# Transposing q and k once, by pairs of heads, in a hybrid attention and convolution layer on one Trainium2 core

## The chip, the core and the metric

The kernel runs on one core of one Trainium2 chip. The metric is the device time of one execution in microseconds (us), the median of three runs. The engines are named as the profile names them: PE is TensorE's matmul stream and PEld its weight loads, DVE is VectorE, ACT is ScalarE, POOL is GpSimd, and SP is the engine whose queue issues nearly all DMAs.

## What is computed

One decoder layer on x of shape (1, 512, 1024) in float32. The reference, cut to what matters here:

```python
xn = rms_norm(h, g_mix_norm)
proj = xn @ w_in                       # 1024 x 2560
q, k, v, u = split(proj, [512, 1024, 1536])
q = partial_rope(to_heads(q)); k = partial_rope(to_heads(k))   # 8 heads of 64
attn = moba_attention(q, k, to_heads(v))       # 512 tokens, blocks of 256: causal softmax attention
conv = conformer_conv(u)               # GLU, causal depthwise conv of 31 taps, LayerNorm, swish
h = h + concat(attn, conv) @ w_out
h = h + square(relu(rms_norm(h) @ w_mlp_in)) @ w_mlp_out
return rms_norm(h)
```

With 512 tokens there are two blocks of 256, and the one earlier block is always chosen, so the attention is plain causal attention.

## The kernel before

Matmul operands are split into a high and a low part of the type fp32r, and a product is the sum of three matmuls (`mm3`, L267): high by high, high by low, low by high. The work has a front (norm, the projections u, q, k, v, the convolution, attention, the output projection y) and an MLP in four chunks (`ff`, `m`). This change is in the front.

The front is written as steps with an engine, a cost, needs and buffers. The class `Plan` lists them: again and again it takes, among the steps that can start, one that starts earliest by its own clock, and among equals the one with the longest tail of work plus a number from the table `BIAS`. Each engine then executes its instructions strictly in the listed order, waiting at each for what that one needs. So the table decides the order, and a late operand holds back everything that is listed behind its reader on that engine. SP is one such engine: a DMA that waits holds back the DMAs behind it.

The steps that matter here, per tile t of 128 tokens:

- `project` makes q, k and v in PSUM (96 matmuls of 512 columns each). `rope` copies a projection to SBUF on ACT (L649) and rotates a quarter of each head on DVE (L659 to L667). For q it writes each head twice, side by side (`dup = 2`), so one q tile has 1024 columns.
- `turn_q` transposes q on PE: for each t two groups of 4 heads (`tpq`, L682); each transposed head has its 64 dimensions in both halves of the partitions. ACT writes the high part `qs` (L687), DVE the low part `ql` (L691), one instruction each per group.
- `turn_k` transposes k by pairs of heads (`tpk`, L702): an even head lies in partitions 0 to 63, an odd one in 64 to 127. For one head `ks` holds the high part in one half of the partitions and the low part in the other; ACT (L707) and DVE (L710) write them for even and odd heads apart, on 64 partitions each.
- `attend`: a score tile (`s`, L775 to L777) is q high and q low against `ks`, 128 rows deep, so that high and low of k are summed in one pass. Then come the row maximum on DVE (`nm`, L782), exp on ACT (`pr`, L784), a reciprocal on DVE (`rs`), a scaling on POOL (L788), transposes of the probabilities on PE (`pt`, L793), their high part on ACT (`ph`, L798) and low part on DVE (`pl`, L802), and the product with v (`o`, L815, L816), which ACT and DVE gather (`ol`, `os`).
- The convolution is spread over DVE (`cs`, L572, one tap each), ACT and POOL. After its last tap `acc` (L589) is joined, PE transposes the sum (`cp`, L849), DVE and POOL normalize it (`bn`, `mv`, `r_ln`, `y` of L871), PE turns it back (`cb`) and ACT applies the swish (`yT`).
- The output projection `y` on PE serves as filler between attention's steps; its second half stands behind the plan, up to the first `ff` matmul.

Weights come by DMA into four `raw` tiles in turn (L446; unit n into tile n mod 4); ACT makes the high part `wh`, DVE or POOL the low part `wl` (L463). Units 12 to 15 are k's, 16 to 19 v's, 20 to 27 those of w_out.

The two lines that make the scores 128 rows deep:

```python
nc.tensor.matmul(p[:, 0:n], qs_tile()[:, h, tok], ks[:, h, 0:n], start=True, stop=False)
nc.tensor.matmul(p[:, 0:n], ql[:, h, tok], ks[:, h, 0:n], start=False, stop=False)
```

Of the kernel before, what the change touches and what calls it, by code (L numbers as in the profile page):

```python
# [17 lines left out]
P = 128  # L18
# [25 lines left out]
DVE_TAPS = (TAPS, 0, TAPS, 11)  # L44

BIAS = {
# [6 lines left out]
}  # L53
PSTEP = 384
PCOLS = 1664
# [116 lines left out]
def hybrid_layer(ctx: ExitStack, tc: tile.TileContext, x, pack, w_in, w_out, g_mlp, w1, w2, g_fin, out):  # L172
    nc = tc.nc
# [12 lines left out]
    def f32(ap):  # L186
        return ap.bitcast(F32)
# [234 lines left out]
    def ps_buffer(name):  # L422
        return plan.buffer("ps", lambda tag: psum.tile([P, 512], F32, tag=tag, name=name))
# [181 lines left out]
    own = [slice(0, HD), slice(HD, P)]  # L605
# [27 lines left out]

    def rope(nm, t, b, ready):


        dup = 2 if nm == "q" else 1
        r = rq[t] if nm == "q" else rs[t]
        qb = qpair[t // 2] if nm == "q" else new_pr(f"{nm}f{t}")

        def tile_of():
            f = get(qb)[t % 2] if nm == "q" else get(qb)
            return f[:, 0:dup * AW].rearrange("p (h u d) -> p h u d", h=NH, u=dup)

        def heads():
            return get(b).rearrange("p (h d) -> p h d", h=NH)

        def copy():
            nc.scalar.activation(tile_of(), heads().unsqueeze(2).to_broadcast([P, NH, dup, HD]), AF.Copy, scale=r)  # L649

        s = plan.step(f"cpy{nm}", "act", 0.69 if dup == 1 else 1.1, copy, needs=[ready], uses=[b, qb])

        def turn():

            two = 2 * HALF
            g = heads()
            cos, sin = (pk[:, c + t * two:c + (t + 1) * two].unsqueeze(1).to_broadcast([P, NH, two]) for c in (C_COS, C_SIN))
            rt = pa.tile([P, NH, two], F32, tag="rope", name=f"rt{nm}{t}", bufs=2)
            nc.vector.scalar_tensor_tensor(rt, g[:, :, 0:two], r, sin, op0=OP.mult, op1=OP.mult)  # L659
            nc.vector.scalar_tensor_tensor(g[:, :, 0:two], g[:, :, 0:two], r, cos, op0=OP.mult, op1=OP.mult)  # L660

            def part(x, n):
                return x[:, :, n * HALF:(n + 1) * HALF].unsqueeze(2).to_broadcast([P, NH, dup, HALF])

            q0, q1 = (tile_of()[:, :, :, n * HALF:(n + 1) * HALF] for n in range(2))
            nc.vector.tensor_tensor(q0, part(g, 0), part(rt, 1), op=OP.subtract)
            nc.vector.tensor_tensor(q1, part(g, 1), part(rt, 0), op=OP.add)  # L667

        s = plan.step(f"rope{nm}", "dve", 1.1, turn, needs=[s], uses=[qb, b])
        return qb, s  # L670

    qready, kready, q_hi = {}, {}, {}

    def turn_q(t, qb, s):
        ts = slice(t * P, (t + 1) * P)
        for a in range(2):
            tp = ps_buffer(f"tpq{t}{a}")

            def flip(a=a, tp=tp):
                for h in range(4):  # L680
                    c = (4 * a + h) * P
                    nc.tensor.transpose(get(tp)[:, h * P:(h + 1) * P], get(qb)[t % 2][:, c:c + P], ident)  # L682

            p = pe_step(f"tq{t}", 4 * 0.11, flip, needs=[s], uses=[qb, tp], chain=False)

            def high(a=a, tp=tp):
                nc.scalar.copy(qs_tile()[:, 4 * a:4 * a + 4, ts], get(tp).rearrange("p (a b) -> p a b", a=4))  # L687

            def low(a=a, tp=tp):
                hs = slice(4 * a, 4 * a + 4)  # L690
                nc.vector.tensor_sub(ql[:, hs, ts], get(tp).rearrange("p (a b) -> p a b", a=4), f32(qs_tile()[:, hs, ts]))  # L691

            hh = plan.step(f"qh{t}", "act", 0.59, high, needs=[p], uses=[tp])
            qready[t, a] = plan.step(f"ql{t}", "dve", 0.69, low, needs=[hh], uses=[tp])

    def turn_k(t, qb, s):
        ts = slice(t * P, (t + 1) * P)
        tp = ps_buffer(f"tpk{t}")

        def flip():  # L700
            for p in range(4):
                nc.tensor.transpose(get(tp)[:, p * P:(p + 1) * P], get(qb)[:, p * P:(p + 1) * P], ident)  # L702

        p = pe_step(f"tk{t}", 4 * 0.11, flip, needs=[s], uses=[qb, tp], chain=False)
        for a in range(2):
            def high(a=a):
                nc.scalar.copy(ks[own[a], a::2, ts], get(tp).rearrange("p (a b) -> p a b", a=4)[own[a]])  # L707

            def low(a=a):
                nc.vector.tensor_sub(ks[own[1 - a], a::2, ts], get(tp).rearrange("p (a b) -> p a b", a=4)[own[a]],  # L710
                                     f32(ks[own[a], a::2, ts]))

            hh = plan.step(f"kh{t}", "act", 0.59, high, needs=[p], uses=[tp])
            kready[t, a] = plan.step(f"kl{t}", "dve", 0.69, low, needs=[hh], uses=[tp])

    plan.slots("pt", ["pt0", "pt1"], 0.0)
    qpair = [plan.buffer("pt", lambda tag, i=i: [pa.tile([P, 2 * AW], F32, tag=f"{tag}{x}", name=f"qf{x}{i}") for x in "hl"])
# [44 lines left out]
    def attend(h):  # L762
# [3 lines left out]
        for qt in range(NT):  # L766
            n = (qt + 1) * P
            tok = slice(qt * P, n)
            sp, tp, pr = ps_buffer(f"s{h}{qt}"), ps_buffer(f"pt{h}{qt}"), new_pr(f"pr{h}{qt}")
            nm, sm, rc = (plan.buffer("st", lambda tag, x=x: perm.tile([P, 1], F32, tag=tag, name=f"{x}{h}{qt}"))  # L770
                          for x in ("nm", "sm", "rs"))

            def scores(sp=sp, n=n, tok=tok):
                p = get(sp)
                nc.tensor.matmul(p[:, 0:n], qs_tile()[:, h, tok], ks[:, h, 0:n], start=True, stop=False)  # L775
                nc.tensor.matmul(p[:, 0:n], ql[:, h, tok], ks[:, h, 0:n], start=False, stop=False)
                nc.tensor.matmul(p[:, tok], identb, maskb, start=False, stop=True)  # L777

            s = pe_step(f"sc{h}", 2 * mm(n) + 0.17, scores, uses=[sp], chain=False, keep=KEEP,
                        needs=[qready[qt, a]] + [kready[t, h % 2] for t in range(qt + 1)] + score_steps[-1:])  # L780
            score_steps.append(s)
            s = plan.step(f"max{h}", "dve", dve_cost(n), lambda sp=sp, nm=nm, n=n: nc.vector.tensor_reduce(  # L782
                get(nm), get(sp)[:, 0:n], AX.X, OP.max, negate=True), needs=[s], uses=[sp, nm])
            s = plan.step(f"exp{h}", "act", 0.45 + 0.00086 * n, lambda sp=sp, nm=nm, sm=sm, pr=pr, n=n: nc.scalar.activation(  # L784
                get(pr)[:, 0:n], get(sp)[:, 0:n], AF.Exp, bias=get(nm), accum_out=get(sm)), needs=[s] + lasts_exp[-1:], uses=[sp, nm, sm, pr])
            lasts_exp.append(s)
            s2 = plan.step(f"rec{h}", "dve", 0.15, lambda sm=sm, rc=rc: nc.vector.reciprocal(get(rc), get(sm)), needs=[s], uses=[sm, rc])
            s = plan.step(f"norm{h}", "pool", 0.32 + 0.00085 * n, lambda pr=pr, rc=rc, n=n: nc.gpsimd.tensor_scalar(  # L788
                get(pr)[:, 0:n], get(pr)[:, 0:n], get(rc), 1.0, op0=OP.mult, op1=OP.mult), needs=[s2], uses=[pr, rc])

            def flip(tp=tp, pr=pr, qt=qt):
                for j in range(qt + 1):
                    nc.tensor.transpose(get(tp)[:, j * P:(j + 1) * P], get(pr)[:, j * P:(j + 1) * P], ident)  # L793

            s = pe_step(f"tp{h}", (qt + 1) * 0.11 + 0.05, flip, needs=[s], uses=[tp, pr], chain=False)

            def high(tp=tp, qt=qt, n=n):
                nc.scalar.copy(key_tiles(get(pt)[0], qt), get(tp)[:, 0:n].rearrange("p (a b) -> p a b", b=P))  # L798

            def low(tp=tp, qt=qt, n=n):  # L800
                ph, pl = get(pt)
                nc.vector.tensor_tensor(key_tiles(pl, qt), get(tp)[:, 0:n].rearrange("p (a b) -> p a b", b=P),  # L802
                                        f32(key_tiles(ph, qt)), op=OP.subtract)

            s = plan.step(f"ph{h}", "act", act_cost(n), high, needs=[s], uses=[tp, pt])
            lows.append(plan.step(f"pl{h}", "dve", dve_cost(n), low, needs=[s], uses=[tp, pt]))
# [599 lines left out]
```

## Time and profile before

| | |
|---|---|
| median of 3 runs | 557.06 us (556.67 to 557.71) |
| the profiled execution | 557.05 us |
| its span, first to last instruction | 555.3 us |
| busy in the span: PE, DVE, ACT, POOL | 541.1, 447.9, 290.9, 214.8 us |
| mean granted TensorE clock | 0.993 |

The time of the profiled execution is 1.75 us over its span, which lies before the first and behind the last instruction. A busy time is the union of an engine's instructions; matmuls overlap, so the distance between two starts is what a matmul costs, not its length in the record. The front ends where the first `ff` matmul starts.

### The profile page before, as it was taken

The page shows a single profiled execution, that of the slowest core. Times are in us where ns is not written, and L with a number is a line of the kernel's source. Part 1 is how long each engine was busy: PE and PEld are TensorE (multiplying, and loading weights), DVE is VectorE, ACT ScalarE, POOL GpSimd, SP SyncE. Part 2 cuts the span into 40 slices and gives each one's busy share as a digit, 9 for nine tenths or more (in the row PEclk, how much of TensorE's full clock was granted, in tenths as well). Part 3 has the DMA queues.
Part 4 walks back from the last instruction along what each step waited for, and adds up shares of the span by engine and source line. Part 5 has one row for each costly group of instructions (what it writes and reads, how often), then busy time and mean ns, then how long its engine had stood idle before and what let it go on. Part 6 is the DMA issues. An engine that isn't in the chain of part 4 may idle for free.

```text
span 555.3 us, 7323 instructions
## 1 busy us (share of the span) xinstructions
PE 541.1 (97%) x2676; PEld 452.1 (81%) x2676; DVE 447.9 (81%) x613; ACT 290.9 (52%) x454; POOL 214.8 (39%) x186
## 2 busy tenths in 40 slices
PE   7999999999999999999999999999999999999993
PEld 6988888777778789988888888888888888888883
DVE  3499999999998577487999475999475999395996
ACT  5847497788883744343553334453244453245354
POOL 3219978777655511250050520240610330800454
PEclk8999999999999999999999999999999999999998
DMA  8552313220204261550027720028620048610003
GB/s 271 156 152 77 99 54 114 76 94 24 74 6 164 95 195 38 185 195 0 1 76 206 248 77 1 1 83 236 210 76 1 0 118 242 186 61 1 1 1 151
DMA packets 58835, 56.18 MB, mean 101 GB/s; under 512 B 1840, under 2 KB 42928, under 8 KB 58800
## 3 DMA queue, kind: packets, MB, share of 16 engines
q1 hardware_dynamic: 58512, 54.68, 31.5%
q10 hardware_dynamic: 288, 1.05, 0.5%
q8 instruction: 21, 0.34, 0.2%
q14 instruction: 14, 0.11, 0.1%
HBM read 53.62 MB, written 2.10 MB: 100 GB/s over the span
## 4 chain that ended last, share of the span: by engine, by line
PE 87%; DVE 8%; issue 1%; ACT 1%; DMA 1%; POOL 0%; SPq 0%; ACTq 0%; POOLq 0%
PE ff L270 11%; PE ff L269 11%; PE ff L271 10%; PE m L270 9%; PE m L269 9%; PE m L271 9%; PE u L270 3%; PE u L269 3%; PE u L271 3%; PE y L269 3%; PE y L271 2%; PE y L270 2%; DVE cs L572 2%; PE q L271 1%; PE q L270 1%
## 5 line engine op out<-in xcount | busy, mean ns | idle before, releaser
L269 PE MATMUL ff<-hTh,wh 128*128 128x512 f32 (+1 forms) x280 | 103.9, 371 | 0.0
L270 PE MATMUL ff<-hTl,wh 128*128 128x512 f32 (+1 forms) x280 | 103.8, 371 | 0.0
L271 PE MATMUL ff<-hTh,wl 128*128 128x512 f32 (+1 forms) x280 | 103.8, 371 | 0.0
L1067 POOL TENSOR_TENSOR r<-r,r 128x1024 f32<-128x1024 f32 x16 | 46.2, 2895 | 141.3 <-DVE wl L1059 136.5
L1075 ACT CAST wh<-raw 128x1024 fp32r<-128x1024 f32 x29 | 30.6, 1055 | 79.0 <-PE ff L270 59.0
L1075 ACT CAST wh<-r 128x1024 fp32r<-128x1024 f32 x40 | 41.7, 1051 | 44.7 <-POOL r L1067 25.7
L1059 DVE TENSOR_TENSOR wl<-raw,wh 128x1024 fp32r<-128x1024 f32 x29 | 39.9, 1375 | 29.4 <-ACT wh L1075 29.2
L1093 DVE TENSOR_TENSOR xr<-xr,m 128x512 f32<-128x512 f32 x96 | 59.5, 677 | 0.9 <-PE m L271 0.9
L269 PEld LDWEIGHTS ff<-hTh,wh 128*128 128x128 f32 x280 | 52.8, 188 | 9.1
L271 PEld LDWEIGHTS ff<-hTh,wl 128*128 128x128 f32 x280 | 52.7, 188 | 9.1
L270 PEld LDWEIGHTS ff<-hTl,wh 128*128 128x128 f32 x280 | 52.8, 188 | 9.0
L1067 POOL TENSOR_TENSOR t<-r,r 128x1024 f32<-128x1024 f32 x8 | 20.1, 2517 | 90.5 <-DMA r<-w 90.5
L572 DVE SCALAR_TENSOR_TENSOR cs<-hin,pk,cs 128x512 f32<-128x512 f32 x68 | 50.9, 749 | 1.0
L1059 DVE TENSOR_TENSOR wl<-r,wh 128x1024 fp32r<-128x1024 f32 x38 | 50.4, 1354 | 0.7 <-ACT wh L1075 0.7
L1110 DVE SCALAR_TENSOR_TENSOR F<-ff,rl 128x512 f32<-128x512 f32 x32 | 21.9, 686 | 33.8 <-ACT rl L1109 33.6
L556 POOL TENSOR_TENSOR acc<-acc,ct 128x512 f32<-128x512 f32 x30 | 44.4, 1479 | 6.5 <-ACT ct L553 4.5
L1109 ACT ACTIVATE rl<-ff 128x512 f32<-128x512 f32 x32 | 19.0, 594 | 49.0 <-PE ff L271 49.0
L553 ACT ACTIVATE ct<-hin,pk 128x512 f32<-128x512 f32 x49 | 32.9, 717 | 2.9 <-DVE hin L536 2.1
L459 ACT CAST wh<-raw 128x1024 fp32r<-128x1024 f32 x21 | 22.0, 1050 | 20.2 <-PE u L270 12.6
L463 DVE TENSOR_TENSOR wl<-raw,wh 128x1024 fp32r<-128x1024 f32 x18 | 29.4, 1633 | 0.9 <-ACT wh L459 0.9
L269 PE MATMUL u<-xh,wh 128*128 128x256 f32 (+1 forms) x88 | 29.6, 337 | 0.0
L270 PE MATMUL u<-xl,wh 128*128 128x256 f32 (+1 forms) x88 | 29.3, 333 | 0.0
(225 smaller groups left out, 1392.4 us busy)
## 6 DMA issues: line engine op xcount, KB each, us to landing
raw<-w SPq DMA_DIRECT2D x32, 512.0 KB, 4.0
r<-w SPq DMA_DIRECT2D x32, 512.0 KB, 5.6
raw<-w_in SPq DMA_DIRECT2D x18, 512.0 KB, 3.6
raw<-w_out SPq DMA_DIRECT2D x8, 512.0 KB, 3.7
xr<-x SPq DMA_DIRECT2D x4, 512.0 KB, 5.7
out<-ot SPq DMA_DIRECT2D x8, 256.0 KB, 2.1
x<-x SPq DMA_DIRECT2D x4, 256.0 KB, 4.8
raw<-w_in SPq DMA_DIRECT2D x4, 256.0 KB, 6.5
```

Of the source, the lines that this page charges most:

```text
L269: nc.tensor.matmul(ps, sh, mh, start=first, stop=False)
L270: nc.tensor.matmul(ps, sh, ml, start=False, stop=False)
L271: nc.tensor.matmul(ps, sl, mh, start=False, stop=last)
L459: nc.scalar.copy(hi, raws[n])
L463: e.tensor_tensor(lo, raws[n], f32(hi), op=OP.subtract)
L553: p = plan.step(f"prod{i}", "act", 0.72, lambda src=src, j=j, ct=ct: nc.scalar.activation(get(ct), src, AF.Copy, scale=wtap(i, j)), needs= ...
L556: s = plan.step(f"tapp{i}", "pool", 1.38, lambda ct=ct: nc.gpsimd.tensor_tensor(get(acc), get(acc), get(ct), op=OP.add), needs=[p, s], use ...
L572: s = plan.step(f"tapd{i}", "dve", 0.78, lambda src=src, j=j, last=last: nc.vector.scalar_tensor_tensor(get(acc) if last else get(cs), src ...
L1059: e.tensor_tensor(lo(), x(), f32(hi()), op=OP.subtract)
L1067: e.tensor_tensor(out(), a(), b(), op=op)
L1075: h = plan.step(f"{kind}h", "act", 1.04, lambda: nc.scalar.copy(get(wb)[0], get(b)), needs=[ready, last.get("high")], uses=[b, wb])
L1093: return plan.step("mev", "dve", dve_cost(n), lambda: nc.vector.tensor_tensor(xt[t][:, cols], xt[t][:, cols], get(b)[:, 0:n], op=op), need ...
```

## The change

q is no longer written twice (`dup = 1`). For each t one group of 4 transposes turns pairs of heads; ACT writes the high part of all four pairs into the even places of `qs` on 128 partitions, DVE the low part into `ql`. An even head then lies right in the lower half only, and the odd head of the pair lies in the upper half of the even head's place. DMAs from SBUF to SBUF carry the parts to their places, 64 partitions by 4 by 128 numbers each, 128 KB: `odd` fills both halves of the odd heads from the upper half of the even places (two DMAs), then `even` copies the lower half over the upper half. That is six DMAs for each t, three for `qs` and three for `ql`.

For k, ACT writes the high part of all pairs into the even places of `ks` and DVE the low part into the odd places, each once on 128 partitions. Then three DMAs follow one another: `side` puts the odd heads' high part away in the upper half of the tile `kf`, `even` moves the even heads' low part into the place that this leaves free, and `odd` brings the high part back from `kf`. Each waits for the one ahead of it. With 24 DMAs for q and 12 for k, 36 are new, all on SP. A score step now needs all parts of its q tile and of all k tiles up to its own.

The core of the diff:

```diff
-        dup = 2 if nm == "q" else 1
+        dup = 1
...
-        for a in range(2):
-            tp = ps_buffer(f"tpq{t}{a}")
...
+        tp = ps_buffer(f"tpq{t}")
+        def flip():
+            for p in range(4):
+                nc.tensor.transpose(get(tp)[:, p * P:(p + 1) * P], get(qb)[t % 2][:, p * P:(p + 1) * P], ident)
...
+        def high():
+            nc.scalar.copy(qs_tile()[:, 0::2, ts], get(tp).rearrange("p (a b) -> p a b", a=4))
...
+        def odd(m):
+            def fn():
+                for half in own:
+                    nc.sync.dma_start(f32(m()[half, 1::2, ts]), f32(m()[own[1], 0::2, ts]))
+            return fn
+        def even(m):
+            return lambda: nc.sync.dma_start(f32(m()[own[1], 0::2, ts]), f32(m()[own[0], 0::2, ts]))
+        oh = plan.step(f"qo{t}", "sp", 1.0, odd(qs_tile), needs=[hh, ll])
+        ol = plan.step(f"qo{t}", "sp", 1.0, odd(lambda: ql), needs=[ll])
+        eh = plan.step(f"qe{t}", "sp", 0.5, even(qs_tile), needs=[oh])
+        el = plan.step(f"qe{t}", "sp", 0.5, even(lambda: ql), needs=[ol])
+        qready[t] = [oh, ol, eh, el]
...
+            nc.scalar.copy(ks[:, 0::2, ts], get(tp).rearrange("p (a b) -> p a b", a=4))
+            nc.vector.tensor_sub(ks[:, 1::2, ts], get(tp).rearrange("p (a b) -> p a b", a=4), f32(ks[:, 0::2, ts]))
+        def side():
+            nc.sync.dma_start(get(qb)[own[1]].rearrange("p (a b) -> p a b", a=4), f32(ks[own[1], 0::2, ts]))
+        def even():
+            nc.sync.dma_start(f32(ks[own[1], 0::2, ts]), f32(ks[own[0], 1::2, ts]))
+        def odd():
+            nc.sync.dma_start(f32(ks[own[0], 1::2, ts]), get(qb)[own[1]].rearrange("p (a b) -> p a b", a=4))
+        s = plan.step(f"ka{t}", "sp", 0.5, side, needs=[hh, p], uses=[qb])
+        e = plan.step(f"kb{t}", "sp", 0.5, even, needs=[s, ll])
+        kready[t] = [e, plan.step(f"kc{t}", "sp", 0.5, odd, needs=[e], uses=[qb])]
...
-                        needs=[qready[qt, a]] + [kready[t, h % 2] for t in range(qt + 1)] + score_steps[-1:])
+                        needs=qready[qt] + [r for t in range(qt + 1) for r in kready[t]] + score_steps[-1:])
```

The table `BIAS` is new for the front; one entry of it, for example:

```diff
-    "norm": 442, "norm3": -13, "os": 124, "ph": 233, "pl": 174, "pl7": 41, "prod": -261, "projq": -117,
+    "mbh": -377, "mbl": -249.6, "mev": -240.1, "mfo": -646, "ml7": 207, "ms1": 261, "norm": 442, "ol": 208,
```

Three places where the order moved. First the SP queue between the weight loads of w_out. Before, only loads stand there (`raw20` is the tile of unit 20):

```order
L446 DMA raw20_1041<-w_out 128x2x512
L446 DMA raw21_1149<-w_out 128x2x512
L446 DMA raw22_1189<-w_out 128x2x512
L446 DMA raw23_1247<-w_out 128x2x512
L446 DMA raw24_1313<-w_out 128x2x512
```

Now the moves of k stand between them (L725 is `side`, L728 `even`, L731 `odd`; `kf1` is tile 1's, and so on; the rows begin behind the `side` of tile 1):

```order
L728 DMA ks_348<-ks_348 64x4x128
L731 DMA ks_348<-kf1_1054 64x4x128
L725 DMA kf2_1086<-ks_348 64x4x128
L445 DMA raw21_1143<-w_out 128x2x512
L728 DMA ks_348<-ks_348 64x4x128
L731 DMA ks_348<-kf2_1086 64x4x128
L445 DMA raw22_1173<-w_out 128x2x512
L725 DMA kf0_1027<-ks_348 64x4x128
L725 DMA kf3_1145<-ks_348 64x4x128
L445 DMA raw23_1231<-w_out 128x2x512
L728 DMA ks_348<-ks_348 64x4x128
L731 DMA ks_348<-kf0_1027 64x4x128
```

Tile 0, which the first score needs, comes third, behind tiles 1 and 2 and two weight loads.

Second, PE at the first score (`s00`). Before, it stands behind 42 of v's 96 matmuls and 28 transposes of q:

```order
L269 MATMUL v1_1134<-wh17_1110,xh_119 128x512
L270 MATMUL v1_1134<-wl17_1111,xh_119 128x512
L271 MATMUL v1_1134<-wh17_1110,xl_120 128x512
L775 MATMUL s00_1242<-ks_348,qs_828 128x128
L776 MATMUL s00_1242<-ks_348,ql_347 128x128
L777 LDWEIGHTS identb_105
```

Now it stands behind 63 of v's matmuls and 16 transposes of q:

```order
L268 MATMUL v1_1130<-wh18_1134,xh_119 128x512
L269 MATMUL v1_1130<-wl18_1135,xh_119 128x512
L270 MATMUL v1_1130<-wh18_1134,xl_120 128x512
L798 MATMUL s00_1285<-ks_348,qs_822 128x128
L799 MATMUL s00_1285<-ks_348,ql_347 128x128
L800 LDWEIGHTS identb_105
```

The first score moved 21 matmuls of v back and 12 transposes forward.

Third, DVE ahead of the first row maximum (`nm`). Before:

```order
L463 TENSOR_TENSOR wl18_1152<-raw18_945,wh18_1151 128x1024
L710 TENSOR_TENSOR ks_348<-tpk3_1159,ks_348 64x4x128 x2
L572 SCALAR_TENSOR_TENSOR cs2_822<-hin2_222,pk_65,cs2_822 128x512 x2
L710 TENSOR_TENSOR ks_348<-tpk0_1200,ks_348 64x4x128 x2
L463 TENSOR_TENSOR wl19_1198<-raw19_999,wh19_1197 128x1024
L691 TENSOR_TENSOR ql_347<-tpq30_1218,qs_828 128x4x128
L782 TENSOR_REDUCE nm03_1252<-s00_1242 128x1
```

Now:

```order
L462 TENSOR_TENSOR wl19_1194<-raw19_992,wh19_1193 128x1024
L722 TENSOR_TENSOR ks_348<-tpk0_1188,ks_348 128x4x128
L688 TENSOR_TENSOR ql_347<-tpq3_1196,qs_822 128x4x128
L722 TENSOR_TENSOR ks_348<-tpk3_1179,ks_348 128x4x128
L571 SCALAR_TENSOR_TENSOR cs2_820<-hin2_222,pk_65,cs2_820 128x512 x4
L462 TENSOR_TENSOR wl20_1261<-raw20_1034,wh20_1260 128x1024
L805 TENSOR_REDUCE nm03_1294<-s00_1285 128x1
```

A pair of low parts of k became one, and more taps (`cs`) stand ahead of the first maximum: between it and the join `acc` of the last channel group there were 22 taps and are now 17, and one `ql` fewer; the last `pl` of 512 columns moved from behind the join to ahead of it. On PE, the product with v of the last head moved ahead of the first `cp`, three `y` matmuls behind it, and the scores are all issued ahead of the first `y`. Behind the first `ff` matmul no engine's order changed.

## Rows read from the trace of the kernel before

**Rows 1.** Busy time by stretch of the front.
```profile
core 0: us, PE busy (x) PEld busy (x) DVE busy (x) ACT busy (x) POOL busy (x), PEclk, DMA share, GB/s
75.00:116.00 41.00, 40.58 (x201) 33.62 (x200) 39.65 (x67) 34.27 (x51) 32.12 (x24) 1.00 0.25 78
116.00:136.00 20.00, 19.89 (x113) 15.92 (x112) 19.87 (x43) 16.05 (x38) 13.56 (x15) 1.00 0.16 53
136.00:158.00 22.00, 20.80 (x137) 16.36 (x135) 21.88 (x62) 20.15 (x59) 14.18 (x20) 1.00 0.14 48
158.00:172.00 14.00, 13.98 (x82) 11.46 (x81) 13.94 (x33) 9.26 (x26) 6.01 (x10) 1.00 0.40 138
172.00:217.00 45.00, 44.94 (x229) 37.25 (x228) 30.91 (x43) 22.47 (x37) 16.08 (x24) 1.00 0.37 111
```
**Rows 2.** PE in order of time: start, length, instruction; transposes of q and k.
```profile
75.05 1.03 PE L682 MATMUL tpq<-ident,qfh 128*128 128x128 f32 x8
75.84 0.48 PE L269 MATMUL q<-wh,xh 128*128 128x512 f32 x1
76.15 0.40 PE L270 MATMUL q<-wl,xh 128*128 128x512 f32 x1
76.38 0.39 PE L271 MATMUL q<-wh,xl 128*128 128x512 f32 x1
...
101.35 0.39 PE L271 MATMUL k<-wh,xl 128*128 128x512 f32 x1
102.15 0.63 PE L702 MATMUL tpk<-ident,kf 128*128 128x128 f32 x4 [0.42 <-DVE kf L667]
```
**Rows 3.** PE: the first score, the first `cp`, the first `ff`.
```profile
116.80 0.22 PE L775 MATMUL s<-ks,qs 128*128 128x128 f32 x1
...
171.81 1.03 PE L849 MATMUL cp<-ident,acc 128*128 128x128 f32 x8
172.60 0.47 PE L815 MATMUL o<-ph,vhl 128*128 128x512 f32 x1
...
173.91 0.44 PE L269 MATMUL y<-wh,mixh 128*128 128x512 f32 x1
...
216.68 0.28 PE L269 MATMUL ff<-hTh,wh 128*128 128x256 f32 x1
```
**Rows 4.** DVE in order of time: first maximum, taps, the last join.
```profile
118.89 0.28 DVE L782 TENSOR_REDUCE nm<-s 128x1 f32<-128x128 f32 x1
119.09 0.75 DVE L572 SCALAR_TENSOR_TENSOR cs<-hin,pk,cs 128x512 f32<-128x512 f32 x1
119.74 0.16 DVE L787 RECIPROCAL rs<-sm 128x1 f32<-128x1 f32 x1
...
170.97 0.67 DVE L589 TENSOR_TENSOR acc<-more,cs 128x512 f32<-128x512 f32 x1
171.57 0.67 DVE L802 TENSOR_TENSOR pl<-pt,ph 128x512 fp32r<-128x512 f32 x1
```
**Rows 5.** Groups of DVE by line: busy us, mean ns, idle before.
```profile
L463 DVE TENSOR_TENSOR wl<-raw,wh 128x1024 fp32r<-128x1024 f32 x18 | 29.4, 1633 | 0.9 <-ACT wh L459 0.9
...
L710 DVE TENSOR_TENSOR ks<-tpk,ks 64x512 fp32r<-64x512 f32 x8 | 5.5, 688 | 0.2
...
L691 DVE TENSOR_TENSOR ql<-tpq,qs 128x512 fp32r<-128x512 f32 x8 | 5.2, 681 | 0.0
```
**Rows 6.** ACT in order of time around the first transposes of k.
```profile
102.82 1.18 ACT L707 CAST ks<-tpk 64x512 fp32r<-64x512 f32 x2 [0.35 <-PE tpk L702]
```
**Rows 7.** DMA issues of the whole span, from the page: KB each, us to landing.
```profile
out<-ot SPq DMA_DIRECT2D x8, 256.0 KB, 2.1
```
**Rows 8.** DMA issues from 27 to 30 us: one load in pieces of 512 bytes.
```profile
raw<-w_in SPq DMA_DIRECT2D x1, 512.0 KB, 3.6
```
**Rows 9.** Busy time by stretch while that load moved (columns as in rows 1).
```profile
28.00:31.00 3.00, 3.00 (x26) 3.00 (x26) 2.76 (x4) 1.15 (x2) 0.00 (x0) 1.00 0.61 175
```
**Rows 10.** SP's queue in order of time: the issue of one DMA.
```profile
0.79 0.38 SPq L284 DMA_DIRECT2D x<-x  x1
```

More of the change, by code (lines that the diff above doesn't have):

```diff
@@ L46 @@
 BIAS = {
[6 rows of a table removed]
+    "ct": 14, "high": 172, "kh3": -79, "low22": -126, "max": -27, "max1": 16, "max5": -83, "max6": -78,
+    "mbh": -377, "mbl": -249.6, "mev": -240.1, "mfo": -646, "ml7": 207, "ms1": 261, "norm": 442, "ol": 208,
[3 rows of a table added]
 }
@@ L675, in turn_q, with low @@
         ts = slice(t * P, (t + 1) * P)
-        for a in range(2):
-            tp = ps_buffer(f"tpq{t}{a}")
[L679 to L694, printed above, removed]
+        tp = ps_buffer(f"tpq{t}")
+        def flip():
+            for p in range(4):
+                nc.tensor.transpose(get(tp)[:, p * P:(p + 1) * P], get(qb)[t % 2][:, p * P:(p + 1) * P], ident)
+        p = pe_step(f"tq{t}", 4 * 0.11, flip, needs=[s], uses=[qb, tp], chain=False)
+        def high():
+            nc.scalar.copy(qs_tile()[:, 0::2, ts], get(tp).rearrange("p (a b) -> p a b", a=4))
+        def low():
+            nc.vector.tensor_sub(ql[:, 0::2, ts], get(tp).rearrange("p (a b) -> p a b", a=4), f32(qs_tile()[:, 0::2, ts]))
+        hh = plan.step(f"qh{t}", "act", 0.59, high, needs=[p], uses=[tp])
+        ll = plan.step(f"ql{t}", "dve", 0.69, low, needs=[hh], uses=[tp])
+        def odd(m):
[10 more added lines that the diff above has]
+        qready[t] = [oh, ol, eh, el]
     def turn_k(t, qb, s):
@@ L704, in turn_k, with high, low @@
         p = pe_step(f"tk{t}", 4 * 0.11, flip, needs=[s], uses=[qb, tp], chain=False)
[L705 to L714, printed above, removed]
+        def high():
+            nc.scalar.copy(ks[:, 0::2, ts], get(tp).rearrange("p (a b) -> p a b", a=4))
+        def low():
+            nc.vector.tensor_sub(ks[:, 1::2, ts], get(tp).rearrange("p (a b) -> p a b", a=4), f32(ks[:, 0::2, ts]))
[5 more added lines that the diff above has]
+            nc.sync.dma_start(f32(ks[own[0], 1::2, ts]), get(qb)[own[1]].rearrange("p (a b) -> p a b", a=4))
+        hh = plan.step(f"kh{t}", "act", 0.59, high, needs=[p], uses=[tp])
+        ll = plan.step(f"kl{t}", "dve", 0.69, low, needs=[hh], uses=[tp])
+        s = plan.step(f"ka{t}", "sp", 0.5, side, needs=[hh, p], uses=[qb])
+        e = plan.step(f"kb{t}", "sp", 0.5, even, needs=[s, ll])
+        kready[t] = [e, plan.step(f"kc{t}", "sp", 0.5, odd, needs=[e], uses=[qb])]
     plan.slots("pt", ["pt0", "pt1"], 0.0)
```

8 rows, old and new, of the table BIAS are left out of this document.

## The prediction

> **What bounds the kernel now.** Read the busy times by stretch first [rows 1]. TensorE is busy nearly all the time, and from the first score (116.80) to the first transposes of the convolution (171.81) VectorE is too: 19.87 of 20, 21.88 of 22 and 13.94 of 14 us. TensorE has room there and only there: 20.80 of 22 us from 136 to 158. The granted clock is 1.00 in every stretch, so neither engine's prices change with it. ScalarE (20.15 of 22 us at most) and GpSimd have room. So three things set the front's end in turn: TensorE up to the first score, VectorE from the first row maximum to the join of the last channel group, TensorE again from there to the MLP. TensorE in order of time shows the marks: scores from 116.80, `cp` at 171.81, `ff` at 216.68 [rows 3]; VectorE in order of time shows the first maximum at 118.89 and the join's end at 170.97 + 0.67 = 171.64, with `cp` right behind it [rows 4]. Behind the first `ff` the order is the old one on every engine, so the MLP takes its 339 us as before and only moves.
>
> The sum is made against the profiled execution, 557.05 us (span 555.3 and 1.75 around it), which is the median of the three runs to 0.01.
>
> **Term 1, TensorE up to the first score.** Twelve of the sixteen transposes of q that go stood ahead of it. Eight took from 75.05 to 75.84, and the matmul behind them 0.31 instead of 0.23 [rows 2]: 0.87 for eight, 0.109 each, 1.31 for twelve. The first transposes of k waited for VectorE's rope: from 101.35 to 102.15 are 0.80 instead of 0.23 [rows 2], 0.57 lost. VectorE has less ahead of that place (three `ql` of 0.68 [rows 5]) and TensorE comes 1.31 earlier; I take the 0.57 as gone. Against that, 21 more matmuls of v stand ahead of the score, 21 x 0.227 = 4.77; that work is only moved, for v has 96 matmuls in either kernel. TensorE is at the first score at 116.80 - 1.31 - 0.57 + 4.77 = 119.7.
>
> **Are the operands there?** This is the one new wait, and its price is in no row. SP issues in order. From the tail of the queue: tile 1's `side`, `even` and `odd`, tile 2's three, tile 0's three, with the loads of units 21, 22 and 23 between. Each `even` waits for its `side` to land and each `odd` for its `even`; what stands behind waits along. Up to the landing of tile 0's last part that is 7 landings in series. The start: tile 1's transposes at 102.15 - 1.31 - 0.57 = 100.3, ScalarE's copy begins 0.67 later and lasts 0.59 (102.82 and half of 1.18) [rows 6], so 101.6. Three issues lie between landings, 0.4 each [rows 10]: 1.2. Tile 0's moves queue behind loads: a load of 512 KB kept the 16 engines busy 0.61 x 3 = 1.8 us [rows 9], less the 0.4 between the issues is 1.4 for the first, and up to 0.7 for the second; I take 1.7 for both. So the operands are there at 104.5 + 7 L, with L the time from the issue of 128 KB to its landing, and TensorE does not wait as long as L is under 2.17.
>
> L is bounded from both sides. The stores of 256 KB, which also start in SBUF, took 2.1 [rows 7]; half as much should not take more. A load of 512 KB in pieces of 512 bytes, the moves' own piece size, took 3.6 [rows 8]; without three quarters of its 1.8 us of data that is 2.25. I take 2.1, the row nearest in source and size: the operands are there at 119.2, half a microsecond ahead of TensorE. The far end, 3.6, would put them at 129.7.
>
> The Trainium skill, page "DMA: Bandwidth & Descriptors", section "Anatomy of one DMA", gives a DMA a fixed 2.0 us and its bytes over 436 GB/s, most of the fixed part being the receipt of the last write; for 128 KB that is 2.3, as an estimate from the page. By it the first score would wait 0.9 us and the sum below would come to 556.3. The 2.1 measured for twice the bytes [rows 7] is under what that rule gives, 2.6; so here the trace speaks for less.
>
> The six moves per tile of q wait in the same way, and the loads of units 17 to 20 stand behind them; q's first transposes stand at 75.05, k's first at 102.15 [rows 2], and v's matmuls, which read unit 17, behind those; 27 us cover the three early rounds of moves of about 4 us each. If that cover fails, v waits and the first score with it.
>
> **Term 2, VectorE from first maximum to join.** VectorE would be free for the maximum at about the old 118.89: four `ks` (0.69) and three `ql` (0.68) go, 4.8, and six taps (119.74 - 119.09 = 0.65 each [rows 4]) and one weight split (1.63 [rows 5]) come, 5.5, and rope writes half as much. So the score decides: the maximum follows it by some 0.6, at 120.3. From there to the join it took 171.64 - 118.89 = 52.75, without idle time [rows 1]. Five taps less are 3.25; one `ql` less and one `pl` of 512 more (0.68 and 0.67) cancel. 120.3 + 52.75 - 3.25 = 169.8, that is 1.8 earlier. TensorE is not in the way: its own work there falls more, by 21 matmuls of v, a group of q's transposes and 3 of `y`, less the last head's product that comes in (1.31), some 4.6 in all. The pieces written on 128 instead of 64 partitions cost nothing extra: 688 ns on 64 and 681 on 128 [rows 5].
>
> **Term 3, from the join to the MLP.** TensorE runs through (44.94 of 45 [rows 1]). The last head's product, 172.60 to 173.91, is out of this stretch, 1.31, and three `y` come in, 0.69: 0.6 less. The weight split that GpSimd gives up stands behind the normalization on VectorE, which has 14 us of room here.
>
> **Nothing for the rest.** ScalarE loses eight copies of 0.59 [rows 6]; it waits for others anyway. The 36 moves are 36 x 0.45 (a quarter of 1.8) = 16 us of DMA time spread over some 50 us whose share was 0.25 [rows 1].
>
> **The sum**: -1.8 - 0.6 = -2.4. From it I take back 0.8. The taps that go were the work with which VectorE bridged the chain from maximum to exp to transposes to low part; 17 are left for 22, and TensorE has no `v` and no `y` between attention's steps for longer. The bounds are 0, the present state, and 3.25, if all five leave holes; present idle of nearly 0 is the nearer row, so a quarter. **557.05 - 2.4 + 0.8 = 555.4 us.**
>
> **Rivals.**
>
> *The chain of moves decides (slower).* If L is over 2.17, each 0.1 costs 0.7 us, since seven landings follow one another and VectorE is full from the first maximum on. At 2.41 the gain is gone, at 2.57 the kernel is 0.2% slower, at 2.7 the score stands at 123.4 and the time is 559.1. For it: the operands would be ready only 0.5 us ahead, and no row shows a move inside SBUF. Against it: 2.1 for double the size.
>
> *The bridge is gone (no change).* If the holes on VectorE take half or all of 3.25 instead of a quarter, the time is 556.2 to 557.9. For it: ScalarE at 20.15 of 22 us was close too, and the chain of a head passes four engines. Against it: VectorE had no holes with TensorE, ScalarE and GpSimd all less than full. The same holds if a low part on 128 partitions at the new stride took twice as long, 4 x 0.69 ahead of the maximum: 557 or so.
>
> *The saving doesn't reach the end.* If the first score comes early but the normalization of the convolution, which now stands in one piece, makes TensorE wait 1 or 2 us behind `cp`, the time is 556.4 to 557.4; 24 `y` matmuls between `cp` and `cb` cover 5.4 us, so I count it with the second rival.
>
> **How the numbers follow.** A measurement of this kernel can tell 0.2%, 1.1 us, from no change: faster is below 555.9, slower above 558.2. The forecast's case, moves in time and at most half of the holes, gets 0.53, and it lies from 553.9 (no holes is 554.6, and the estimates of the score's place and of the 0.6 to the maximum may be 0.7 too high together) to 555.9. The second and third rival together with the milder part of the first, L between 2.2 and 2.55, get 0.28. L above that gets 0.19. The range reaches from 553.9 to 558.4, L up to 2.6, and leaves out the worse tail. Faster 0.53, same 0.28, slower 0.19.
>
> **What would show it.** Right: the moves of 128 KB land within 2.2 us; PE has no idle time at the first scores; the first maximum comes near 120.3, the join ends near 170.5, the first `ff` starts 1.5 to 2 us earlier. Wrong: idle time of PE ahead of `s` released by a DMA (first rival); VectorE busy clearly under 99% between first maximum and join (second); PE idle ahead of `cb` (third). If the first score came before 119 with little idle, my constant of 104.5 would be too high, and the order of v alone would decide.

## The result, and the profile after

The changed kernel takes 560.35 us (median of 5 runs, 559.56 to 562.41) against 557.06 (5 runs too): ratio 1.0067, 95% interval 1.0051 to 1.0082. It is 0.67% slower; 555.4 was forecast. The profiled execution took 560.01 us with a span of 558.3.

The front's start differs from execution to execution by up to 2.5 us, so stretches are compared from one instruction, the first matmul of q, whose row in the kernel before is this (PE in order of time: start, length, instruction):

```profile
58.04 0.39 PE L269 MATMUL q<-wh,xh 128*128 128x512 f32 x1
```

In that kernel the fourth group of scores (the first of 512 columns) follows the work ahead of it without a stop:

```profile
123.77 0.23 PE L777 MATMUL s<-maskb,identb 128*128 128x128 bf16 x1
123.81 0.48 PE L775 MATMUL s<-ks,qs 128*128 128x512 f32 x1
```

The same view of the changed kernel, with q's first matmul, the first and the fourth group of scores, and `cp`:

```profile
57.58 0.39 PE L268 MATMUL q<-wh,xh 128*128 128x512 f32 x1
...
118.92 0.39 PE L270 MATMUL v<-wh,xl 128*128 128x512 f32 x1
121.40 0.30 PE L798 MATMUL s<-ks,qs 128*128 128x128 f32 x1 [2.09 <-issue]
...
125.38 0.27 PE L816 MATMUL pt<-ident,pr 128*128 128x128 f32 x1
127.91 0.47 PE L798 MATMUL s<-ks,qs 128*128 128x512 f32 x1 [2.26 <-DMA qs<-qs]
128.79 0.49 PE L799 MATMUL s<-ks,ql 128*128 128x512 f32 x1 [0.40 <-DMA ql<-ql]
...
174.95 1.91 PE L872 MATMUL cp<-ident,acc 128*128 128x128 f32 x16
```

PE stops twice, for 2.25 us ahead of the first score (118.92 + 0.23 is 119.15) and for 2.5 ahead of the fourth group; neither stop was there before (the first score in [rows 3]). VectorE in order of time, and the view of its waits from 117 to 130:

```profile
121.92 0.29 DVE L805 TENSOR_REDUCE nm<-s 128x1 f32<-128x128 f32 x1 [3.47 <-PE s L800]
...
129.69 0.89 DVE L805 TENSOR_REDUCE nm<-s 128x1 f32<-128x128 f32 x2 [3.07 <-PE s L800]
...
174.12 0.69 DVE L588 TENSOR_TENSOR acc<-more,cs 128x512 f32<-128x512 f32 x1
```

```profile
DVE nm L805 <- PE s L800: 6.5, 2, 3.5
```

VectorE, which had no idle time here before [rows 1], waits 3.5 and 3.1 us for scores. Why the scores were late stands on SP's queue, in order of time (start and length of an issue; an instruction waits for the landing of the one it needs, and what stands behind waits along):

```profile
101.23 0.60 SPq L725 DMA_DIRECT2D kf<-ks  x1
103.65 0.60 SPq L728 DMA_DIRECT2D ks<-ks  x1
106.00 0.59 SPq L731 DMA_DIRECT2D ks<-kf  x1
106.70 0.59 SPq L725 DMA_DIRECT2D kf<-ks  x1
107.79 0.38 SPq L445 DMA_DIRECT2D raw<-w_out  x1
109.18 0.60 SPq L728 DMA_DIRECT2D ks<-ks  x1
112.21 0.59 SPq L731 DMA_DIRECT2D ks<-kf  x1
112.90 0.56 SPq L445 DMA_DIRECT2D raw<-w_out  x1
113.50 1.98 SPq L725 DMA_DIRECT2D kf<-ks  x2
115.58 0.60 SPq L445 DMA_DIRECT2D raw<-w_out  x1
118.96 0.60 SPq L728 DMA_DIRECT2D ks<-ks  x1
121.33 0.59 SPq L731 DMA_DIRECT2D ks<-kf  x1
...
126.39 0.59 SPq L700 DMA_DIRECT2D ql<-ql  x1
```

`kf<-ks` is a `side` (L725), `ks<-ks` an `even` (L728), `ks<-kf` an `odd` (L731), `raw` a load. Each step of tile 1 follows 2.4 us after the one before. Tile 0's `side` (113.50) goes out behind the load of unit 22 (112.90) and takes 5.39 us to land, so its `even` can only start at 118.96. That `even` lands at 121.31, and the first score starts at 121.40. Behind it come `odd`, q's four odd moves, tile 3's `even` and q's two even moves. The last of these are issued at 125.40 and 126.39 and land at 127.78 and 128.74, where the two matmuls of the fourth group had been waiting. A move with no load beside it takes, from issue to landing (the DMA issues from 121 to 127.5: x count, KB each, median us to landing):

```profile
qs<-qs SPq DMA_DIRECT2D x3, 128.0 KB, 2.4
ql<-ql SPq DMA_DIRECT2D x3, 128.0 KB, 2.4
```

The stretches of all kernels below, in us, worked out from starts of rows like those above, one profiled execution of each (the fourth group is counted from q's first matmul, too):

| kernel | q to first score | q to 4th group | first max. to last join's start | `cp` to `ff` | q to `ff` |
|---|---|---|---|---|---|
| before | 58.76 | 65.77 | 52.08 | 44.87 | 158.64 |
| the change | 63.82 | 70.33 | 52.20 | 44.86 | 162.23 |
| no moves | 61.56 | 65.49 | 49.03 | 44.85 | 156.72 |
| loads behind | 61.74 | 68.32 | 53.59 | 44.81 | 161.51 |
| one more move | 69.40 | 75.89 | 51.87 | 44.85 | 167.80 |
| k by engines | 61.77 | 65.84 | 48.81 | 44.83 | 157.60 |
| `side` on ScalarE | 61.56 | 67.34 | 53.03 | 44.84 | 160.70 |
| load 22 on ScalarE | 62.11 | 68.60 | 52.24 | 44.84 | 160.55 |
| load 22 on SP | 64.22 | 70.69 | 52.21 | 44.81 | 162.61 |
| woven | 61.99 | 66.00 | 49.02 | 44.85 | 157.23 |
| woven, copies first | 62.11 | 66.14 | 49.04 | 44.05 | 156.58 |
| the same, `even` first | 61.56 | 65.50 | 49.03 | 44.03 | 155.90 |

From `ff` to the end of the last instruction of an engine every kernel takes 334.2 to 334.3 us; the span ends 4.2 to 4.5 later, with the last stores.

### The profile page after: what moved, and what is told of

Its sections match the earlier page's. It is cut to its first block, busy times and chain, and to the rows that moved or that the text cites. A ratio compares the mean times of both kernels' runs of the same rounds, so it can differ in the third digit from the quotient of the medians.

```text
span 558.3 us, 7353 instructions
## 1 busy us (share of the span) xinstructions
PE 540.0 (97%) x2660; PEld 451.6 (81%) x2660; DVE 447.2 (80%) x607; ACT 283.2 (51%) x446; POOL 207.9 (37%) x184
## 3 DMA queue, kind: packets, MB, share of 16 engines
q10 hardware_dynamic: 288, 1.05, 0.7%
## 4 chain that ended last, share of the span: by engine, by line
PE 68%; DVE 3%; ACT 1%; issue 1%; POOL 0%; ACTq 0%
PE ff L268 10%; PE ff L269 10%; PE ff L270 10%; PE m L269 9%; PE m L268 9%; PE m L270 9%; PE y L268 3%; PE y L270 3%; PE y L269 2%; DVE pl L825 1%; DVE nm L805 1%; PE pt L816 0%; DVE xr L1116 0%; PE th L985 0%; PE o L838 0%
## 5 line engine op out<-in xcount | busy, mean ns | idle before, releaser
L1090 POOL TENSOR_TENSOR r<-r,r 128x1024 f32<-128x1024 f32 x16 | 44.0, 2762 | 146.4 <-DVE wl L1082 137.1
L1082 DVE TENSOR_TENSOR wl<-raw,wh 128x1024 fp32r<-128x1024 f32 x29 | 41.5, 1430 | 24.8 <-ACT wh L1098 24.7
L462 DVE TENSOR_TENSOR wl<-raw,wh 128x1024 fp32r<-128x1024 f32 x20 | 30.1, 1504 | 2.2 <-ACT wh L458 1.2
```

The source lines that it names most:

```text
L462: e.tensor_tensor(lo, raws[n], f32(hi), op=OP.subtract)
L1082: e.tensor_tensor(lo(), x(), f32(hi()), op=OP.subtract)
L1090: e.tensor_tensor(out(), a(), b(), op=op)
```

## The experiments

Theory A: the moves' landings, in series on SP, make the first and the fourth group of scores late; the rest went about as forecast. Theory B: the new order itself leaves holes on VectorE, the prediction's second rival. In every kernel PE, VectorE, ScalarE and GpSimd keep the order of the change unless the text says otherwise.

**No moves.** All 36 DMAs out; each head reads the place of its pair's even head, so the output is not the reference's.

```diff
-                    nc.sync.dma_start(f32(m()[half, 1::2, ts]), f32(m()[own[1], 0::2, ts]))
+                pass
...
-                nc.tensor.matmul(p[:, 0:n], qs_tile()[:, h, tok], ks[:, h, 0:n], start=True, stop=False)
+                nc.tensor.matmul(p[:, 0:n], qs_tile()[:, h - h % 2, tok], ks[:, h - h % 2, 0:n], start=True, stop=False)
...
```

> All 36 moves are left out, and with them the copies of q and k in the other half; every head reads the place of the even head of its pair. The order on PE, VectorE, ScalarE and GpSimd is that of the change. Theory A (SP's chain of landings makes the first scores late, and nothing else was wrong): PE reaches the first score at 119.1 instead of 121.4, there is no stop at the fourth score group, VectorE takes about 49 us instead of 52.2 from the first maximum to the last join, and the time is 554.5 to 555.5. Theory B (the new order leaves holes on VectorE, because the taps that bridged the chain of attention are gone): the first score comes earlier but the stretch stays near 52, and the time is 557.5 or more.

Measured: 554.81 us, ratio to before 0.9964 (0.9949 to 0.9979). No score waits, and VectorE is full again (busy time by stretch, columns as in rows 1):

```profile
119.00:129.00 10.00, 10.00 (x61) 7.93 (x60) 9.90 (x25) 7.82 (x24) 6.71 (x9) 1.00 0.12 46
129.00:136.00 7.00, 6.28 (x39) 4.58 (x38) 6.98 (x19) 6.83 (x18) 4.98 (x5) 1.00 0.16 61
136.00:158.00 22.00, 20.84 (x143) 16.79 (x141) 21.86 (x65) 20.27 (x62) 12.58 (x22) 1.00 0.10 35
```

The same stretches of the changed kernel:

```profile
119.00:129.00 10.00, 5.25 (x26) 3.62 (x24) 4.70 (x11) 4.68 (x11) 3.31 (x4) 1.00 0.54 139
129.00:136.00 7.00, 7.00 (x45) 5.68 (x45) 6.21 (x17) 4.75 (x15) 3.35 (x5) 1.00 0.29 75
136.00:158.00 22.00, 20.13 (x133) 15.78 (x132) 21.85 (x62) 20.76 (x59) 13.69 (x20) 1.00 0.15 49
```

Theory B falls. The moves cost 162.23 - 156.72 = 5.51 us from q to `ff`: 2.26 ahead of the first score, and 3.17 between first maximum and join, where the fourth group waits.

**Loads behind.** SP issues the loads of units 22 and 23 after the last move.

```diff
     order = plan.run()
+    late = [s for s in order if s["kind"] in ("load22", "load23")]
+    order = [s for s in order if s["kind"] not in ("load22", "load23")]
+    i = next(i for i, s in enumerate(order) if s["kind"] == "kc3") + 1
+    order[i:i] = late
```

> SP issues the loads of units 22 and 23 behind the last move of k instead of between them; nothing else moves. Theory A, with the queue as the cause of 3 us of it: the side move of tile 0 lands 2.4 us after its issue instead of 5.4, tile 0's even move lands near 117.7, PE reaches the first score at 119.1 without a stop, but the fourth score group still waits for q's moves until about 125.2 (127.9 in the change); the time is about 557.7, 2.6 under the change. Theory B: within 1 us of the change, since VectorE's holes only move.

Measured: 559.10 us, ratio 1.0038 (1.0024 to 1.0053); direction right, size wrong. The two `side` moves took 3.3 us and not 2.4, although no load was in flight (see the last section), and the first score comes 2.08 earlier than in the change. The fourth group comes 2.0 earlier, but `ff` only 0.72. What took the rest back is TensorE's clock (busy time by stretch, columns as in rows 1):

```profile
125.00:128.00 3.00, 0.55 (x2) 0.27 (x2) 0.79 (x2) 0.46 (x3) 1.57 (x2) 1.00 0.66 169
128.00:131.00 3.00, 3.00 (x12) 2.47 (x13) 0.96 (x3) 0.78 (x2) 0.59 (x1) 0.56 0.88 275
131.00:134.00 3.00, 3.00 (x16) 2.25 (x16) 2.79 (x8) 1.67 (x5) 1.72 (x2) 0.87 0.69 262
```

PE stood while the fourth group waited (0.55 busy of 3 us), and from about 128 the granted clock is at its lower level, 1.2 GHz; the matmuls of v stand 0.43 us apart instead of 0.23 (PE in order of time):

```profile
127.14 0.47 PE L798 MATMUL s<-ks,qs 128*128 128x512 f32 x1 [2.32 <-DMA qs<-qs]
...
129.81 0.63 PE L270 MATMUL v<-wh,xl 128*128 128x512 f32 x1
130.24 0.41 PE L798 MATMUL s<-ks,qs 128*128 128x256 f32 x1
```

Two stretches of 3 us at 0.56 and 0.87 lose 3 x 0.44 + 3 x 0.13 = 1.7 us of full clock, an estimate and of the size of the 1.3 missing. In the profiled execution of the change the clock stayed at 1.00 through stops as long as this; the five executions of the change have mean clocks of 0.988 to 0.996, the longest one the lowest and the profiled one the highest.

**One more move.** Tile 0's `side` twice, in series.

```diff
+            if t == 0:
+                nc.sync.dma_start(get(qb)[own[1]].rearrange("p (a b) -> p a b", a=4), f32(ks[own[1], 0::2, ts]))
             nc.sync.dma_start(get(qb)[own[1]].rearrange("p (a b) -> p a b", a=4), f32(ks[own[1], 0::2, ts]))
```

> Tile 0's side move is made twice, so that one more landing stands in SP's chain ahead of the first score; nothing else changes. Theory A: first score and fourth score group come one landing, 2.4 us, later, and so does the end: 562.5 to 563.5. Theory B: VectorE's holes take most of it up: under 561.5.

Measured: 564.59 us, ratio 1.0127 (1.0105 to 1.0149), more than expected. The first score comes 5.58 later than in the change, `ff` 5.57: what is late at the score is late at the end, one for one. 2.9 of this is the landing that was added, which makes `even` go out later. The rest, which the expectation did not have, is that the load of unit 23 now went out 1.05 us ahead of tile 0's `even`, where 3.4 lay between the two in the change (SP's queue):

```profile
121.23 0.62 SPq L445 DMA_DIRECT2D raw<-w_out  x1
122.28 0.60 SPq L730 DMA_DIRECT2D ks<-ks  x1
127.34 0.59 SPq L733 DMA_DIRECT2D ks<-kf  x1
```

`even` at 122.28 took 5.05 us to land instead of 2.35.

**K by engines.** k's 12 moves out; ScalarE and VectorE write k's parts as before, q's 24 moves stay.

```diff
-            nc.scalar.copy(ks[:, 0::2, ts], get(tp).rearrange("p (a b) -> p a b", a=4))
+            for a in range(2):
+                nc.scalar.copy(ks[own[a], a::2, ts], get(tp).rearrange("p (a b) -> p a b", a=4)[own[a]])
...
```

> The moves of k alone are undone: ScalarE and VectorE write k's parts across the halves in pieces of 64 partitions, as in the kernel before (four instructions more on each of the two); q keeps its 24 moves, and every other instruction keeps its place. Theory A (k's moves are the late ones, because three follow one another for each tile): the first score starts when PE reaches it, and of the 2.5 us at the fourth score group at most 1.5 remain, from q's last moves behind the loads of units 22 and 23: 554.8 to 556.3. Theory B (q's moves do as much harm, by their number): 558 or more.

Measured: 555.12 us, ratio 0.9973 (0.9963 to 0.9983). Without k's moves q's 24 do next to no harm (fourth group at 65.84 against 65.49): those of the last tile go out from 113.42 on instead of 121.97, since SP is not kept by k's. It takes k's 12, three in series per tile, to make them late.

**`side` on ScalarE.** Tile 0's and 3's `side` issued by ScalarE, the load of unit 23 behind the last move.

```diff
-            nc.sync.dma_start(get(qb)[own[1]]
+            (nc.scalar if t in (0, 3) else nc.sync).dma_start(get(qb)[own[1]]
...
```

> The side moves of tiles 0 and 3 are issued by ScalarE, into its own queue, at about the time at which SP issued them; the load of unit 22 keeps its place on SP's queue and is in flight at that time, the load of unit 23 goes behind the last move. Theory Q (the 5.4 us were a place in a queue: a queue's transfers go one behind the other): the two side moves land 2.4 to 3 us after their issue though the load is in flight, tile 0's even lands near 118.5, and the time is 556 to 557.5. Theory S (the 16 DMA engines are shared, whatever the queue): they take 4 to 5.5 us, and the time is 558.5 to 560.

Measured: 558.70 us, ratio 1.0038 (1.0025 to 1.0051). The first score is on time (61.56). The question of the queue was not answered: ScalarE issued tile 0's `side` at 110.73, ahead of the load, and it landed in 2.40; tile 3's, issued 0.55 ahead of the load and on another queue than it, took 4.23, but a move there took 3.3 without any load, too. The time lies in the range that the expectation gave to shared engines, but the wait at the fourth group makes it, so it decides nothing. The fourth group still waits 1.85 (67.34 against 65.49), and behind that stop the clock was 0.77 from 125 to 128 and 0.66 from 128 to 131.

**Load 22 on ScalarE, and on SP.** The load of unit 23 goes behind the last move in both; the load of unit 22 is issued by ScalarE in one, and stays on SP in the other.

```diff
-                nc.sync.dma_start(raws[n].rearrange(
+                (nc.scalar if n == 22 else nc.sync).dma_start(raws[n].rearrange(
...
```

> The change with the load of unit 23 behind the last move and the load of unit 22 issued by ScalarE into its own queue at about the old time, so that no load stands on SP's queue among the moves. What is asked is the time to landing of the side and even moves of tile 0. Theory Q (they wait in SP's queue behind the load): about 3.3 and 3.0, as without any load. Theory S (the engines are shared by the queues): 4.5 to 5.5, as with the load on SP's queue.

> The same, but the load of unit 22 keeps its place on SP's queue, ahead of the two side moves; only the load of unit 23 goes behind the last move. Both theories: the side moves take 4.5 to 5.4, and tile 0's even move, which has only the end of that load beside it, 2.4 to 3. The run gives the level against which the one with the load on ScalarE's queue is read.

Measured, one run each: 557.82 and 560.12 us. With the load on SP the `side` moves took 5.40 and 4.48, as in the change, so it is the load of unit 22 that delays them and not that of unit 23. With the load on ScalarE's queue they took 3.94 and 3.56, nearer to the 3.3 without a load. But that load also went out earlier (110.07 instead of 112.98; counted from q's first matmul, 2.7 us), since ScalarE had no landing to wait for; so it stays open how far a queue of its own or the earlier time helped. The first score came 2.11 earlier than with the load on SP.

**Woven.** SP's tail in an order in which other issues fill the waits, with the loads of units 22 and 23 behind the moves.

```diff
+    line = "ka0 qo3 ka3 kc2 qo3 kb0 qe3 kb3 qe3 kc0 kc3 load22 load23".split()
+    tail = [s for s in order if s["kind"] in line]
+    order = [s for s in order if s["kind"] not in line]
+    at = 0
+    for k in line:
+        m = tail.pop(next(i for i, s in enumerate(tail) if s["kind"] == k))
+        at = max([at] + [i + 1 for i, s in enumerate(order) if any(s is n for n in m["needs"])])
+        order.insert(at, m)
+        at += 1
```

> SP's tail in another order: tile 0's side, q's moves and tile 3's side are issued into the waits of the other chains, and the loads of units 22 and 23 behind all; the other engines keep the order of the change. Theory A: tile 0's even move lands near 117.5 and the last move near 121, ahead of PE (119.1 and 123.2), so no score waits: 554.5 to 555.5, faster than both kernels. Theory B: 557.5 or more.

Measured: 554.78 us, ratio 0.9961 (0.9947 to 0.9976), faster than the kernel before and 1.0% under the change, with the same 36 moves. Loads behind moves alone gave 559.10, so most of it is the weaving. SP's queue:

```profile
109.43 0.59 SPq L725 DMA_DIRECT2D kf<-ks  x1
110.11 1.26 SPq L696 DMA_DIRECT2D qs<-qs  x2
111.47 0.59 SPq L725 DMA_DIRECT2D kf<-ks  x1
112.15 1.60 SPq L731 DMA_DIRECT2D ks<-kf  x1
113.81 1.28 SPq L696 DMA_DIRECT2D ql<-ql  x2
115.13 0.63 SPq L728 DMA_DIRECT2D ks<-ks  x1
...
118.20 1.59 SPq L731 DMA_DIRECT2D ks<-kf  x2
119.83 17.16 SPq L445 DMA_DIRECT2D raw<-w_out  x5
```

The last move is out at 119.2 instead of 127.1 (this execution starts 1.3 us earlier), and the loads follow.

**Woven, copies first.** Beside that, ScalarE makes the fourth `yT` copy ahead of the first Silu.

```diff
+    i, j = (next(i for i, s in enumerate(order) if s["kind"] == k) for k in ("sw0", "yst3"))
+    order.insert(i, order.pop(j)) if not any(s["kind"] == "cb3" for s in order[i:]) else order.insert(j, order.pop(i))
```

> The woven order of the moves, and beside it ScalarE makes its fourth copy of the normalized tiles ahead of loading the table of Silu and of the first Silu, instead of behind them. Theory A (PE stands 0.9 to 1.0 us at 186 because that copy frees its bank late, and that took back what the move of work out of this stretch saved): 553.9 to 554.1, 0.7 to 0.9 under the woven order alone. Rival: the saved time comes back at the next wait, since Silu itself starts 0.8 later: 554.8, the same.

Measured: 554.15 us, ratio 0.9958 (0.9947 to 0.9970). What it mends, in the changed kernel (PE, then ScalarE, in order of time):

```profile
185.80 0.40 PE L270 MATMUL y<-wh,mixl 128*128 128x512 f32 x1
187.05 0.50 PE L268 MATMUL y<-wh,mixh 128*128 128x512 f32 x1 [0.86 <-ACT yT L905]
```

```profile
184.42 1.28 ACT L908 ACT_TABLE_LOAD   x1
185.72 0.81 ACT L908 ACTIVATE yT<-yT,pk 128x512 f32<-128x512 f32 x1
186.44 0.56 ACT L905 COPY yT<-cb 128x512 f32<-128x512 f32 x1
```

The bank that PE needs is read out only behind the table's load and a Silu. With the copy first, `cp` to `ff` falls by 0.80 to 44.05; the intervals of the two kernels overlap, so the gain is seen in the stretch and not in the times alone.

**The same, `even` first.** `kb0` one place earlier in the list: `kc2 kb0 qo3` for `kc2 qo3 kb0`.

> The kernel with woven moves and ScalarE's copy ahead of Silu, and one step earlier on SP: tile 0's even move goes ahead of q's second pair of odd moves. With the woven order PE stopped for about 0.4 us ahead of the first score, since that even move landed 118.18 (0.09 ahead of the score). Theory A: it lands over 1 us earlier, the stop goes, and the end comes 0.3 to 0.4 earlier: 553.7 to 553.9. Rival: q's moves, now later, stop the fourth score group instead: 554.2 or more.

Measured: 553.35 us, ratio 0.9948 (0.9929 to 0.9966), the lowest median here and 0.35 under the range expected; its interval overlaps with that of the kernel before it, so this gain, too, is seen in the stretches. First score (61.56) and fourth group (65.50) now stand where they stand without any move: 36 moves cost nothing, if each lands before it is needed.

## Why the prediction was wrong

*Term 1, TensorE's own way to the first score: right.* 2.9 us more was forecast. Without waits, q to first score is 61.56 against 58.76: 2.80 more.

*Are the operands there: wrong, and here the prediction failed.* It said that they are there at 104.5 + 7 L with L = 2.1, half a microsecond ahead of PE. The mechanism, which is the first rival, was right, and its threshold of 2.17 was passed: L is 2.35 for a move with no load beside it. The prediction took the 2.1 of the stores [rows 7] and argued that half as many bytes would not take more; they did. The Trainium skill, page "DMA: Bandwidth & Descriptors", section "Anatomy of one DMA", gives a DMA of the kind that GpSimd issues a fixed 2.0 us and the bytes over 436 GB/s, 2.3 as an estimate for 128 KB. By that figure the trace agrees for these moves, which SP issues, and not for the stores. Two terms beside L were also off. An issue of a move takes 0.59 to 0.63, not the 0.4 of a load [rows 10]. Moves beside loads were priced at 1.7; in the series up to tile 0's `even`, the excess of tile 2's `even` (3.02) and of tile 0's `side` (5.39) over 2.35 is 0.67 + 3.04 = 3.7; about 1 of the 3.04 is not the load's, since `side` took 3.3 with the loads behind. In return the first score, head 0's, needs only six landings, for it does not read what `odd` writes: it starts at 121.40, and tile 0's `odd` is issued at 121.33.

*A step that was left out.* The prediction asked for the operands of the first score alone, and had VectorE full from then on. The fourth group needs q's six moves and tile 3's three, and most of them stood on SP behind tile 0's. PE was there 4 us behind the first score, and the moves 6.5. That cost 3.17 us, more than the first stop (2.26). By the first rival's own price, 0.7 per 0.1 of L, L = 2.35 gives 556.7; the fourth group is most of what is missing to 560.35.

*Term 2, VectorE: right.* First maximum to join was to fall by 3.25; in the kernel without moves it falls by 3.05 (52.08 to 49.03), and the maximum follows the score by 0.44, where 0.6 was taken.

*The 0.8 taken back for holes, and the second rival: the size was too high.* 0.2 is gone, not 0.8; VectorE has 21.86 of 22 us.

*Term 3: the 0.6 did not come.* `cp` to `ff` is 44.86 against 44.87: PE's stop of 1.0 us behind ScalarE's fourth copy took it back. That is the third rival's kind of wait, though behind `cb`'s first transposes (182.19) rather than ahead of them, and of about the size that rival named.

*The sum without its failed step.* -1.8 - 0.6 + 0.8 = -1.6 was forecast from q to `ff`; without moves it is -1.92, with the woven moves -1.41. So 555.4 is near where the changed order goes once the moves are in time (554.78). That it comes so close is in part luck: the 0.6 too much taken back for holes and the 0.6 of term 3 that did not come cancel.

## What to carry to other kernels

Where an in-order queue waits for landings, count the landings in series up to every consumer that stops an engine, and not up to the first alone; then fill the waits with issues that are ready, and put loads that nobody needs yet behind them. Here that alone made a slower kernel into a faster one, with the same instructions on every other engine. Where an engine is full from some point on, a wait ahead of it reaches the end one for one.

## What was not expected of the hardware

- A move of 128 KB between halves of the partitions lands 2.3 to 2.5 us after its issue if nothing is beside it, also when four follow at 0.65 us; with a load of 512 KB on SP's queue beside it, 4.3 to 5.4 for the `side` moves, and 2.9 to 3.5 for tile 2's `even`, which follows its load by 1.4 to 1.5 us.
- About 55 us behind q's first matmul a move takes 2.9 to 4.3 us in every kernel that has one there, with no load in flight too (3.31 and 3.30 in the kernel with the loads behind). The trace of that kernel has something else on the DMA engines there, a packet of 16 KB that the profile names `instruction` (DMA queues from 114 to 115; then the stretches behind it, columns as in rows 1):

```profile
q8 instruction: 1, 0.02, 8.0%
```

```profile
115.00:116.00 1.00, 1.00 (x6) 0.84 (x5) 0.96 (x2) 0.37 (x1) 0.92 (x2) 1.00 0.73 182
116.00:117.00 1.00, 1.00 (x7) 0.80 (x6) 0.94 (x2) 0.00 (x0) 1.00 (x1) 1.00 0.14 32
```

8.0% of 16 engines in 1 us is 1.3 us of one engine. From 116 to 117 the engines stand nearly empty, and the moves issued at 113.38 to 114.75 land only at 117.06 to 118.05, as if one engine's share of each came late. Every kernel has such a packet there. Another one comes 29.6 to 29.8 us behind q's first matmul in all kernels with q's moves, and the move issued at 28.3 to 28.4 takes 3.7 to 4.0 in each of them, though the next load is issued only 2.9 us behind it. No run moved these packets, so the cause is read from the trace and not shown by an experiment.
- A stop of PE of some 2 us was followed by a lowered clock in three kernels (in two stretches of 3 us each: 0.56 and 0.87 with the loads behind, 0.77 and 0.66 with `side` on ScalarE, 0.56 and 0.87 with load 22 on SP), and by none in the profiled executions of the change and of load 22 on ScalarE. Why one and not the other was not tried. What it costs depends on what stands behind: the kernel with the loads behind lost about 1.3 us in that way, while with load 22 on SP the clock fell right behind the first stop, where PE had the fourth group's wait ahead of it, and `ff` came 98.39 us behind the first score, as in the change (98.41).
